# A two-layer hybrid trunk on one core: when modulation, weight splitting and the last output jobs stand in a planned order

## The chip, the cores and the metric

One core of a Trainium2 chip runs one program that holds the whole trunk. The metric is device time in microseconds (us). Engines are named as in the profile: PE is TensorE's matmul side and PEld its weight loads, DVE is VectorE, ACT ScalarE, POOL GpSimd, SP SyncE, whose queue issues nearly every DMA.

## What is computed

2048 rows of width 1024 pass two layers (batch 1). Each layer normalises and modulates its input, projects it, runs two mixers, projects the concatenated result back, normalises that and adds it through a gate:

```python
c_act = jax.nn.silu(c)
for i in range(2):
    shift, scale, gate = split(c_act @ ada_w[i] + ada_b[i], 3)
    h = rms_norm(x, norm_pre[i]) * (1 + scale) + shift
    if i == 0: y = concat([rwkv7_mix(...), short_conv_mix(...)]) @ ev_w_out
    else:      y = concat([conformer_conv_mix(...), mamba2_ssd_mix(...)]) @ od_w_out
    x = x + gate * rms_norm(y, norm_post[i])
```

`rwkv7_mix` is a recurrence over positions (computed in chunks of 64), `conformer_conv_mix` a causal convolution of 31 taps with a layer norm behind it, `mamba2_ssd_mix` a chunked scan. All is float32. A matmul of full accuracy is made of three fast ones: both operands are split into a high part and a rest, and high x high, high x rest and rest x high are added up.

## The kernel before

**Tiling.** The rows are cut into four blocks of 512. Layer 0 has 33 projection jobs for each block and layer 1 has 25; each layer also has 32 output jobs, for an output projection of 16 row tiles by 2 column halves. A job is one PSUM tile `pp` of 128x512 and 24 matmuls (3 products x 8 slices of the inner dimension; the dt job has 16). PE works through a written list of jobs; every other piece of work (evacuations, the recurrences, transposes, norms, loads) is spread between the matmuls.

**The planner.** A single-threaded Python planner emits the instructions in program order. All side work sits in generators in eight queues (`bg`, `quick`, `ev`, `aux`, `post`, `tail`, `urgent`, `slow`); `tick` gives each one step every 2 matmuls in layer 0 and every 4 in layer 1. `later(n, f)` puts a store off by n ticks. In layer 0 (`gated`) a `Clock` models when each engine would be done: `now` is the matmuls' time, `chain` the end of the latest chain, and every DMA issue adds 3.5 us to `chain`; the next matmul starts at the later of the two. A queue's step is held while the engines' modelled lag behind `now` is above a bound (`LAG`, 2 to 3 us; `SLOWV`, 8 us, for the slow queue).

**The work that the change touches.** `modulation` loads a 128x1024 tile of `ada_w` (tile `h`), multiplies it with silu(c) and sums it on DVE into one column of `mod`, followed by one or two 128x1 operations. The first 16 tiles are done in `first_block`; the other 32 (8 for layer 0's gate, 24 for layer 1) are in the slow queue. `gate_row` turns the gate's column into the row tile `gp` that output jobs multiply with. `presplit` reads layer 1's input weights and both layers' output weights, splits them (ACT casts, POOL subtracts) and stores both parts in DRAM (`wo`, `w1`, `wdt`), from where later jobs load them ready. `w_out` loads 16 parts of output weights of one column half into one of two big `act` tiles, as 8 DMAs of 512 KB. `out_jobs` evacuates output jobs: the first half of a row tile is kept in DRAM (`od`), the second fetches it and the row tile `x`, norms, adds and stores. `hblock` norms and transposes the next block's input. `conf_out` ends the conformer branch of a block: four transposes of the convolved channels (`co`) with statistics, four transposes back (`xn`), and per channel group a scaled copy `cs`, a tanh `pr`, two products on DVE, a cast `yh`, and the store of both parts to DRAM as `y`, from which the output jobs of that block load their operand `w`. In the last block the order ends with output jobs of tiles 8 to 11, then of tiles 12 to 15, which need that block's own `y`.

**What sets the order.** The order of jobs is written out by hand in `tile_trunk` (`put` places a list behind the n-th projection job of a block); where a side step lands between them follows from the queues, the clock, and waits for a tile to come free (`take`, which makes the planner wait until `free`; tiles taken from a pool without it make the issuing engine wait on the chip).

Of the kernel before, what the change touches and what calls it, by code (L numbers as in the profile page):

```python
# [9 lines left out]
F32 = mybir.dt.float32  # L10
# [8 lines left out]
P = 128  # L19
D = 1024  # L20
KT = D // P
HALF = 1024
BL = 512
# [125 lines left out]
class Trunk:  # L149
# [83 lines left out]
    def take(self, name, shape, bufs=1, busy=None, dtype=F32):  # L233

        ring = self.rings.setdefault((id(self.t) if name != "tr" else 0, name), [])
        while len(ring) >= bufs and id(ring[-bufs]) in self.inuse:
            yield busy
        t = self.tr.tile(shape, F32, name=name) if name == "tr" else self.t.tile(shape, dtype, name=name, bufs=bufs)
# [27 lines left out]
    def setup(self):  # L266
# [46 lines left out]
        self.kept, self.parted = set(), set()  # L313
# [27 lines left out]
    def gate_row(self, l):  # L341
# [7 lines left out]
        for hb in range(2):  # L349
            ps = yield from self.take("tr", [P, BL], 2)  # L350
# [83 lines left out]
    def run_jobs(self, order, feed):  # L434

        more = lambda n: any(not callable(o) and o[2] == order[n][2] for o in order[n + 1:])
        for n, o in enumerate(order):
# [16 lines left out]
            feed.fetch()  # L454
            if job.mm:
# [210 lines left out]
    def out_jobs(self, l, ts, dh, key):  # L666

        def evac(t, ps):
# [4 lines left out]
            else:  # L673
                x = self.x_rows(l, t, self.xp.tile([P, D], F32, name="x"))
# [35 lines left out]
            def store():  # L710
                self.nc.sync.dma_start(out=self.x1[t] if l == 0 else self.out[t * P:(t + 1) * P], in_=x)
                self.x_done[l].add(t)

# [570 lines left out]
    def conf_out(self, b, st):  # L1284
# [24 lines left out]
        for g in range(4):  # L1309
# [4 lines left out]
            w = yield from self.take("cs", [P, BL])  # L1314
# [239 lines left out]
def tile_trunk(ctx, tc, I, out, T):  # L1554
# [3 lines left out]
    with ExitStack() as e:  # L1558
# [6 lines left out]
        k.slow += [k.modulation(0, range(16, 24), 1), k.modulation(1, range(24), 1), k.gate_row(0)]  # L1565
# [16 lines left out]
        split_w = [(I["w_in1"][j], k.w1[j]) for j in range(24)] + [(I["w_in1"][24], k.wdt)]  # L1582
        put(blocks[1], 0, [lambda: k.slow.append(k.presplit(split_wo(0) + split_w + split_wo(1)))])
# [12 lines left out]
        for b, (l, ts) in enumerate([(0, tiles(2)), (0, tiles(3)), (1, tiles(0)), (1, tiles(1))]):  # L1596
            last = b == NB - 1
            load, jobs = zip(*[outs(l, ts if not dh or not last else range(4, 4 * NB), dh) for dh in range(2)])
            for p, o in zip(at, [load[0], *jobs[0], load[1], *jobs[1][:4]]):
                put(blocks[b], p, [o])  # L1600
            if not last:
# [64 lines left out]
```

## Time and profile before

| | |
|---|---|
| median of 3 runs | 2455.23 us (2452.19 to 2456.57) |
| the profiled execution's own time | 2446.16 us |
| its span | 2444.4 us, mean granted clock 0.947 |
| PE busy | 2208.9 us, 90% of the span, 13408 matmuls |
| PEld busy | 1728.7 us, 71% |
| DVE busy | 1753.1 us, 72% |
| ACT busy / POOL busy | 811.4 us, 33% / 593.3 us, 24% |
| first matmul of each block of layer 0 | 25.6, 364.9, 693.7, 1007.1 us |
| first matmul of each block of layer 1 | 1404.7, 1646.1, 1867.2, 2089.5 us |

Read it as an engine that is nearly always busy, PE, with the time between its busy stretches gathered in a few stages; those stages, not the shares over the whole span, decide what a change is worth. "Granted clock" is the share of TensorE's full clock.

### The profile page before, as it was taken

Reading aid. Unit: us, or ns where it says so; the run is one execution under the profiler, and the core shown is the slowest. Engines: PE = TensorE matmul, PEld = TensorE weight load, DVE = VectorE, ACT = ScalarE, POOL = GpSimd, SP = SyncE. Lnnn points to the kernel's source line nnn. Section 1 sums busy time; section 2 is a strip of 40 time slices with the busy share of each in tenths; the row PEclk is TensorE's granted clock in tenths of the full one; section 3 lists DMA queues with packets and bytes.
Section 4 is the critical chain, followed back from the end, with each engine's and each line's share of the span. In section 5 each row is a group of like instructions: output and inputs, shape, how many; then the busy total and the mean of one; then the engine's idle time right before and its main releaser. Section 6 shows DMA issues by size and latency. Waiting matters only on the chain. (4 is left out here: it accounts for less than half of the span.)

```text
span 2444.4 us, 36532 instructions
## 1 busy us (share of the span) xinstructions
PE 2208.9 (90%) x13408; PEld 1728.7 (71%) x13408; DVE 1753.1 (72%) x3340; ACT 811.4 (33%) x1731; POOL 593.3 (24%) x792
## 2 busy tenths in 40 slices
PE   6688889898988989989999979999999999999957
PEld 4566667676766767667777667877778787878836
DVE  6797897867857778565377443689589859967961
ACT  4334223433233322221222432353443525252221
POOL 2544535335253140221042310210020012002021
PEclk9788989999898999999999989999999999999978
DMA  8675676776776544544788678867877786787756
GB/s 302 223 254 179 216 260 226 234 251 226 248 237 215 199 122 159 190 129 139 254 292 268 235 266 296 301 226 254 293 252 248 243 298 207 267 275 276 244 178 232
DMA packets 232390, 575.18 MB, mean 235 GB/s; under 512 B 20498, under 2 KB 70418, under 8 KB 232212
## 3 DMA queue, kind: packets, MB, share of 16 engines
q1 hardware_dynamic: 232068, 572.59, 69.2%
q8 instruction: 106, 1.74, 0.3%
q14 instruction: 72, 0.59, 0.1%
q10 hardware_dynamic: 144, 0.26, 0.0%
HBM read 436.91 MB, written 135.86 MB: 234 GB/s over the span
## 5 line engine op out<-in xcount | busy, mean ns | idle before, releaser
L111 PE MATMUL pp<-act,w 128*128 128x512 f32 x7000 | 1797.8, 408 | 47.0 <-DMA w<-y 22.0
L111 PEld LDWEIGHTS pp<-act,w 128*128 128x128 f32 x7000 | 1312.5, 193 | 343.5 <-DMA w<-y 22.4
L111 DVE SCALAR_TENSOR_TENSOR co<-u,cfw,co 128x512 f32<-128x512 f32 x480 | 345.3, 754 | 6.1 <-ACT co L111 5.8
L111 POOL TENSOR_SCALAR ss<-ss 128x1 f32<-128x1 f32 x80 | 27.0, 338 | 639.5 <-DVE ss L111 463.2
L111 POOL TENSOR_TENSOR x<-x 128x512 fp32r<-128x512 f32 x80 | 109.0, 1376 | 134.8 <-ACT x L111 134.2
L111 POOL TENSOR_SCALAR sp<-S,PL 128x64 f32<-128x64 f32 x128 | 66.2, 531 | 194.1 <-DVE S L111 193.8
L111 DVE TENSOR_TENSOR pr<-X,BK 128x2 f32<-128x2 f32 (+30 forms) x248 | 101.6, 410 | 6.2
L111 ACT ACTIVATE tA<-pp 128x512 f32<-128x512 f32 x64 | 38.1, 596 | 203.4 <-PE pp L111 201.5
L111 POOL TENSOR_TENSOR w<-x,w 128x512 fp32r<-128x512 f32 x57 | 83.6, 1479 | 56.6 <-ACT w L111 56.4
L111 DVE TENSOR_REDUCE X<-pr 128x1 f32<-128x2 f32 (+30 forms) x248 | 86.5, 349 | 6.1
L111 ACT ACTIVATE q<-pp,cp 128x512 f32<-128x512 f32 x65 | 44.7, 688 | 128.6 <-PE pp L111 106.8
L111 DVE TENSOR_TENSOR UV<-ch,scal 64x128 f32<-64x128 f32 x128 | 36.9, 289 | 58.3 <-PE ch L111 56.3
L111 POOL COPY q<-carry 128x1 f32<-128x1 f32 (+1 forms) x84 | 38.6, 460 | 155.0 <-DVE tG L111 65.0
L111 POOL COPY carry<-q 128x1 f32<-128x1 f32 (+1 forms) x84 | 22.3, 265 | 221.8 <-ACT q L111 172.3
L111 POOL TENSOR_TENSOR x<-x,yo 128x512 f32<-128x512 f32 x32 | 48.5, 1516 | 104.0 <-DVE yo L111 91.5
L111 DVE TENSOR_TENSOR ss<-oss 128x1 f32<-128x1 f32 x32 | 6.0, 189 | 92.1 <-ACT tA L111 92.0
L111 ACT CAST x<-x 128x512 fp32r<-128x512 f32 x80 | 46.6, 616 | 72.6 <-DMA w<-w 19.5
L111 DVE SCALAR_TENSOR_TENSOR tG<-pp,derived,q 128x512 f32<-128x512 f32 x65 | 48.4, 744 | 30.9 <-ACT q L111 30.5
L111 DVE TENSOR_TENSOR act<-tr,act 128x256 fp32r<-128x256 f32 (+1 forms) x120 | 51.3, 436 | 24.1 <-ACT act L111 23.4
L111 PE MATMUL tr<-cc,h 128*128 128x128 f32 x224 | 39.6, 293 | 31.8 <-ACT h L111 28.6
L111 DVE STREAM_TRANSPOSE BK<-SC 32x1024 f32<-32x1024 f32 x32 | 63.8, 1993 | 0.5
L111 ACT ACTIVATE yo<-pp 128x512 f32<-128x512 f32 x32 | 19.1, 597 | 127.9 <-PE pp L111 112.6
(273 smaller groups left out, 3164.6 us busy)
## 6 DMA issues: line engine op xcount, KB each, us to landing
w<-w SPq DMA_DIRECT2D x450, 512.0 KB, 4.3
w<-y SPq DMA_DIRECT2D x128, 512.0 KB, 4.4
act<-wo SPq DMA_DIRECT2D x88, 512.0 KB, 6.1
x<-in_w_in_dram SPq DMA_DIRECT2D x58, 512.0 KB, 5.5
w<-x SPq DMA_DIRECT2D x96, 256.0 KB, 3.4
h<-in_ada_w_dram SPq DMA_DIRECT2D x32, 512.0 KB, 4.9
y<-yh SPq DMA_DIRECT2D x64, 256.0 KB, 3.1
wo<-x SPq DMA_DIRECT2D x64, 256.0 KB, 3.5
```

The lines of the kernel that those rows point to most:

```text
L111: return f(*args, **kw)
```

## The change

Seven edits:

1. `take` handles the `x` tiles (2 buffers), which `presplit` and the second halves of output jobs now take and free, so that the planner waits for one.
2. `presplit` puts its four stores off by 8 ticks (`later(STORE, ...)`), and works on one weight tile at a time.
3. `run_jobs` sets the clock's `chain` back to 0 ahead of each job's matmuls, so that the 3.5 us of a weight fetch no longer move the modelled matmuls.
4. The 32 slow modulation tiles and layer 0's `gate_row` start in block 1, behind the first 21 items of `presplit`; the rest of `presplit` follows them. The order of `presplit` is now: layer 0's output weights, dt, input weights 16 to 23, 12 to 15, then 0 to 11, then layer 1's output weights.
5. `gate_row` waits for a PSUM tile in another way (`busy` True).
6. `conf_out`'s tile `cs` has two buffers.
7. In layer 1's last block, four output jobs (tiles 4 to 7, first half) stand inside the block where there were eight; twelve output jobs (tiles 8 to 11 of half 0, 4 to 11 of half 1) stand between its last projection job and the eight of tiles 12 to 15, where there were eight. One load of output weights (`again`) goes.

```diff
     def take(self, name, shape, bufs=1, busy=None, dtype=F32):
-        ring = self.rings.setdefault((id(self.t) if name != "tr" else 0, name), [])
+        ring = self.rings.setdefault((id(self.t) if name not in ("tr", "x") else 0, name), [])
...
     def presplit(self, tiles):
         for src, parts in tiles:
-            lo = self.raw(src)
+            lo = yield from self.take("x", [P, D], 2)
+            self.nc.sync.dma_start(out=lo if len(src.shape) == 2 else lo.rearrange("p (k t) -> p k t", k=src.shape[1]), in_=src)
...
-            hi = self.xp.tile([P, D], F32, name="x")
+            hi = yield from self.take("x", [P, D], 2)
             yield True
-            yield
             for z in range(2):
                 own = slice(z * BL, (z + 1) * BL)
                 self.split(hi[:, own].bitcast(F32R), lo[:, own].bitcast(F32R), lo[:, own])
-                yield
-            for z in range(2):
-                for i, part in enumerate((hi, lo)):
-                    self.nc.sync.dma_start(out=parts[z][:, i], in_=part[:, z * BL:(z + 1) * BL])
-                self.parted.add(id(parts[z]))
+            def store(parts=parts, hi=hi, lo=lo):
+                for z in range(2):
...
+                self.stored += 1
+                self.free(hi)
+                self.free(lo)
+            self.later(STORE, store)
+            self.begun_split += 1
+            yield
+            while self.stored < self.begun_split:
                 yield
@@ run_jobs
             feed.fetch()
+            self.clock.chain = 0.0
             if job.mm:
@@ out_jobs
-                x = self.x_rows(l, t, self.xp.tile([P, D], F32, name="x"))
+                x = self.x_rows(l, t, (yield from self.take("x", [P, D], 2, "blocked")))
@@ conf_out
-            w = yield from self.take("cs", [P, BL])
+            w = yield from self.take("cs", [P, BL], 2)
@@ tile_trunk
-        k.slow += [k.modulation(0, range(16, 24), 1), k.modulation(1, range(24), 1), k.gate_row(0)]
...
-        put(blocks[1], 0, [lambda: k.slow.append(k.presplit(split_wo(0) + split_w + split_wo(1)))])
+        put(blocks[1], 0, [lambda: k.slow.extend(
+            [k.presplit(split_wo(0) + split_w[:13]), k.modulation(0, range(16, 24), 1), k.modulation(1, range(24), 1), k.gate_row(0), k.presplit(split_w[13:] + split_wo(1))])])
...
-        again, first = outs(1, range(8, 4 * NB), 0)
-        blocks[-1] += [again, *jobs[1][4:8], *first[:4]] + [j for two in zip(jobs[1][8:], first[4:]) for j in two]
+        load, jobs = zip(*[outs(1, range(4, 4 * NB), dh) for dh in range(2)])
+        for p, o in zip((1, 5, 10, 15, 18), [load[0], *jobs[0][:4]]):
+            put(blocks[-1], p, [o])
+        blocks[-1] += [load[1], *jobs[0][4:8], *jobs[1][:8]] + [j for two in zip(jobs[0][8:], jobs[1][8:]) for j in two]
```

**DVE, block 0, the chain ahead of its first recurrence step.** `h,mod_107<-h,gp` is one modulation tile, `tG`, `tA` and `wal` belong to the recurrence's preparation. Before:

```order
L111 SCALAR_TENSOR_TENSOR h,mod_107<-h,gp 128x1024
L111 SCALAR_TENSOR_TENSOR tG<-yp,derived,q 128x512
L111 TENSOR_TENSOR mod_107<-mod_107,cp 128x1
L111 TENSOR_TENSOR gs_109<-mod_107,cp 128x1
L111 SCALAR_TENSOR_TENSOR h,mod_107<-h,gp 128x1024
L111 TENSOR_TENSOR mod_107<-mod_107,cp 128x1
L111 TENSOR_TENSOR gs_109<-mod_107,cp 128x1
L111 SCALAR_TENSOR_TENSOR h,mod_107<-h,gp 128x1024
L111 TENSOR_TENSOR wal_865<-w2a_832,wh_863 64x128
```

Of the change, the same place:

```order
L111 SCALAR_TENSOR_TENSOR tD<-tG,cp,tD 128x512
L111 TENSOR_SCALAR scal<-kss 64x2 x4
L111 SCALAR_TENSOR_TENSOR tG<-yp,derived,q 128x512
L111 TENSOR_TENSOR wal_852<-w2a_845,wh_850 64x128
L111 TENSOR_TENSOR wal_852<-w2a_845,ah_851 64x128
L111 TENSOR_SCALAR tA<-tA 128x512
L111 SCALAR_TENSOR_TENSOR tA<-reset,tA 128x512
```

The modulation tiles between `tG` and `wal` are gone. Before, 31 of the 32 stand in block 0 and one at the start of block 1; now 8 stand in block 1 and 24 in block 2. With them `gate_row(0)` moves from the first jobs of block 1 to the end of block 2. Elsewhere in layer 0 few instructions change their places on DVE and ACT; the splits of layer 1's output weights now end ahead of the last layer 0 job instead of among layer 1's first jobs, and 56 small matmuls of layer 0's recurrence and its transposes stand behind the last layer 0 job instead of 16.

**PE, the end of the last block.** `co` and `xn` are `conf_out`'s transposes, `act_61` and `act_62` the two operand tiles of output weights and of the block. Before, from the last of the eight jobs that stood ahead of tiles 12 to 15:

```order
L111 MATMUL pp<-act_62,w 128x512 x18
L111 MATMUL tr<-cc,co 128x128 x2
L111 MATMUL pp<-act_62,w 128x512 x12
L111 MATMUL tr<-cc,co 128x128 x4
L111 MATMUL pp<-act_62,w 128x512 x10
L111 MATMUL tr<-cc,co 128x128 x4
L111 MATMUL tr<-cc,xn 128x128 x16
L111 MATMUL pp<-act_61,w 128x512 x24
```

Of the change:

```order
L111 MATMUL tr<-cc,co 128x128 x4
L111 MATMUL pp<-act_62,w 128x512 x20
L111 MATMUL tr<-cc,xn 128x128 x4
L111 MATMUL pp<-act_62,w 128x512 x12
L111 MATMUL tr<-cc,xn 128x128 x4
L111 MATMUL pp<-act_62,w 128x512 x12
L111 MATMUL tr<-cc,xn 128x128 x4
L111 MATMUL pp<-act_62,w 128x512 x24
L111 MATMUL tr<-cc,xn 128x128 x4
L111 MATMUL pp<-act_62,w 128x512 x44
L111 MATMUL pp<-act_61,w 128x512 x24
```

The four groups of `xn` transposes stood in one bunch with no output job between them or behind them; now 112 matmuls of output jobs stand between the last `co` and the first job (`act_61`, the last row) that needs the block's own `y`.

**ACT, the same place.** `cs`, `pr` and `yh` are the three ACT operations per channel group, `tA,oss` an output job's second half. Before:

```order
L111 ACTIVATE tA,oss<-pp 128x512 x4
L111 ACTIVATE cs<-tr,cp 128x512
L111 ACTIVATE pr<-tr,derived 128x512
L111 CAST yh<-cs 128x512
L111 ACTIVATE cs<-tr,cp 128x512
L111 ACTIVATE pr<-tr,derived 128x512
L111 CAST yh<-cs 128x512
```

Of the change:

```order
L111 ACTIVATE tA,oss<-pp 128x512 x4
L111 ACTIVATE cs<-tr,cp 128x512
L111 ACTIVATE pr<-tr,derived 128x512
L111 ACTIVATE cs<-tr,cp 128x512
L111 CAST yh<-cs 128x512
L111 ACTIVATE pr<-tr,derived 128x512
L111 ACTIVATE tA,oss<-pp 128x512
L111 CAST yh<-cs 128x512
L111 ACTIVATE tA,oss<-pp 128x512 x2
```

The second `cs` now stands ahead of the first `yh`, and evacuations of output jobs stand between the groups.

## Rows read from the trace of the kernel before

**Rows 1.** The page's 40 slices of the span: busy tenths and granted clock.

```profile
PE   6688889898988989989999979999999999999957
DVE  6797897867857778565377443689589859967961
PEclk9788989999898999999999989999999999999978
```

**Rows 2.** Windows by stage: us; busy of PE, PEld, DVE, ACT, POOL; clock; DMA.

```profile
46.00:145.00 99.00, 74.34 (x343) 57.57 (x341) 76.69 (x137) 33.63 (x65) 41.01 (x45) 0.76 0.70 254
145.00:198.00 53.00, 44.98 (x240) 36.97 (x241) 48.60 (x102) 18.95 (x35) 22.79 (x23) 0.89 0.72 257
198.00:307.00 109.00, 98.79 (x809) 72.96 (x808) 91.33 (x191) 45.20 (x92) 56.42 (x68) 0.94 0.57 191
307.00:365.00 58.00, 46.86 (x262) 37.29 (x261) 56.81 (x122) 13.02 (x25) 18.46 (x17) 0.87 0.76 266
365.00:694.00 329.00, 303.03 (x2403) 226.83 (x2401) 245.69 (x499) 105.57 (x195) 130.04 (x166) 0.94 0.72 238
694.00:1007.00 313.00, 287.56 (x2128) 217.06 (x2126) 225.17 (x462) 88.61 (x164) 87.90 (x130) 0.93 0.55 179
1007.00:1405.00 398.00, 378.20 (x2685) 288.98 (x2680) 245.88 (x508) 109.44 (x212) 95.14 (x153) 0.97 0.65 219
1405.00:1490.00 85.00, 68.44 (x275) 53.85 (x275) 35.23 (x64) 30.48 (x73) 13.64 (x10) 0.86 0.78 269
...
2341.00:2390.00 49.00, 11.89 (x52) 8.28 (x51) 21.53 (x37) 9.63 (x16) 8.74 (x15) 0.63 0.45 146
2390.00:2436.00 46.00, 45.93 (x192) 37.54 (x192) 6.88 (x12) 7.16 (x18) 6.09 (x9) 0.95 0.73 262
```

**Rows 3.** DVE groups by shape, 95 to 385 us: count | busy us, mean ns.

```profile
L111 DVE SCALAR_TENSOR_TENSOR h<-h,gp 128x1024 f32<-128x1024 f32 x31 | 43.0, 1388 | 7.0 <-DMA h<-in_ada_w_dram 7.0
L111 DVE TENSOR_TENSOR mod<-mod,cp 128x1 f32<-128x1 f32 x31 | 12.8, 414 | 0.1
L111 DVE TENSOR_TENSOR gs<-mod,cp 128x1 f32<-128x1 f32 x15 | 4.5, 300 | 0.1
L111 DVE SCALAR_TENSOR_TENSOR gs<-mod,cp 128x1 f32<-128x1 f32 x8 | 3.0, 378 | 0.0
```

**Rows 4.** Tiles h and mod, 90 to 390 us: ns min/median/max, first and last start.

```profile
L111 DVE SCALAR_TENSOR_TENSOR h<-h,gp x31: 1161/1216/2335, 94.5 to 378.8; 128x1024 f32<-128x1024 f32 x31
L111 DVE TENSOR_TENSOR mod<-mod,cp x31: 105/152/1247, 96.4 to 380.8; 128x1 f32<-128x1 f32 x31
```

**Rows 5.** POOL groups by shape, 95 to 385 us, the largest.

```profile
L111 POOL TENSOR_TENSOR w<-x,w 128x512 fp32r<-128x512 f32 x50 | 74.0, 1492 | 52.5 <-ACT w L111 52.4
```

**Rows 6.** PE's waits, 25 to 365 us, the largest: us in total, times, longest.

```profile
PE tr L111 <- DVE tE L111: 18.7, 2, 10.7
```

**Rows 7.** PE's waits, 365 to 1405 us, first and last of the eleven over 1.5 us.

```profile
PE tr L111 <- DVE yy L111: 16.0, 4, 6.3
...
PE tr L111 <- DVE kss L111: 1.6, 1, 1.6
```

**Rows 8.** PE's waits, 1405 to 1490 us.

```profile
PE tr L111 <- DMA x<-in_w_out_dram: 6.9, 1, 6.9
PE pp L111 <- DMA w<-w: 4.5, 2, 3.0
```

**Rows 9.** Tile S, 1300 to 1405 us: 16 of its DVE updates, two a step.

```profile
L111 DVE SCALAR_TENSOR_TENSOR S<-ch,PL,sp x16: 273/276/285, 1339.7 to 1373.1; 128x64 f32<-128x64 f32 x16
```

**Rows 10.** ACT's timeline, 2356 to 2384 us: start, us, operation, idle before.

```profile
2358.03 0.78 ACT L111 ACTIVATE cs<-tr,cp 128x512 f32<-128x512 f32 x1 [6.07 <-PE tr L111]
...
2365.47 0.78 ACT L111 ACTIVATE cs<-tr,cp 128x512 f32<-128x512 f32 x1 [3.90 <-DMA y<-cs]
...
2372.35 0.78 ACT L111 ACTIVATE cs<-tr,cp 128x512 f32<-128x512 f32 x1 [3.33 <-DMA y<-cs]
...
2379.28 0.78 ACT L111 ACTIVATE cs<-tr,cp 128x512 f32<-128x512 f32 x1 [3.34 <-DMA y<-cs]
```

**Rows 11.** PE's timeline, 2340 to 2391 us: the last row.

```profile
2390.07 1.22 PE L111 MATMUL pp<-act,w 128*128 128x512 f32 x2 [21.98 <-DMA w<-y]
```

**Rows 12.** DVE's timeline, 2300 to 2346 us: the convolution's taps.

```profile
2305.42 24.97 DVE L111 SCALAR_TENSOR_TENSOR co<-u,cfw,co 128x512 f32<-128x512 f32 x37
...
2343.47 0.74 DVE L111 SCALAR_TENSOR_TENSOR co<-u,cfw,co 128x512 f32<-128x512 f32 x1
```

More of the change, by code (lines that the diff above doesn't have):

```diff
@@ L233, in take @@
     def take(self, name, shape, bufs=1, busy=None, dtype=F32):
-        ring = self.rings.setdefault((id(self.t) if name != "tr" else 0, name), [])
+        ring = self.rings.setdefault((id(self.t) if name not in ("tr", "x") else 0, name), [])
         while len(ring) >= bufs and id(ring[-bufs]) in self.inuse:
             yield busy
-        t = self.tr.tile(shape, F32, name=name) if name == "tr" else self.t.tile(shape, dtype, name=name, bufs=bufs)
+        t = {"tr": self.tr, "x": self.xp}[name].tile(shape, F32, name=name) if name in ("tr", "x") else self.t.tile(shape, dtype, name=name, bufs=bufs)
         ring.append(t)
@@ L349, in gate_row @@
         for hb in range(2):
-            ps = yield from self.take("tr", [P, BL], 2)
+            ps = yield from self.take("tr", [P, BL], 2, True)
             for q in range(4):
@@ L410, in presplit @@
                 self.split(hi[:, own].bitcast(F32R), lo[:, own].bitcast(F32R), lo[:, own])
-                yield
-            for z in range(2):
-                for i, part in enumerate((hi, lo)):
-                    self.nc.sync.dma_start(out=parts[z][:, i], in_=part[:, z * BL:(z + 1) * BL])
-                self.parted.add(id(parts[z]))
+            def store(parts=parts, hi=hi, lo=lo):
+                for z in range(2):
+                    for i, part in enumerate((hi, lo)):
+                        self.nc.sync.dma_start(out=parts[z][:, i], in_=part[:, z * BL:(z + 1) * BL])
+                    self.parted.add(id(parts[z]))
+                self.stored += 1
+                self.free(hi)
+                self.free(lo)
+            self.later(STORE, store)
+            self.begun_split += 1
+            yield
+            while self.stored < self.begun_split:
                 yield
@@ L712, in store @@
                 self.x_done[l].add(t)
+                self.free(x)
             self.later(STORE, store)
@@ L1595, in tile_trunk @@
         at = 1, 3, 5, 7, 9, 9, 12, 13, 15, 16
[L1596 to L1599, printed above, removed]
+        for b, (l, ts) in enumerate([(0, tiles(2)), (0, tiles(3)), (1, tiles(0))]):
+            load, jobs = zip(*[outs(l, ts, dh) for dh in range(2)])
+            for p, o in zip(at, [load[0], *jobs[0], load[1], *jobs[1]]):
                 put(blocks[b], p, [o])
-            if not last:
-                put(blocks[b], at[-1], ahead(1, b + 1, 2))
+            put(blocks[b], at[-1], ahead(1, b + 1, 2))
             if b == 1:
                 put(blocks[1], 23, [lambda: k.slow.append(k.gate_row(1))])
-        again, first = outs(1, range(8, 4 * NB), 0)
-        blocks[-1] += [again, *jobs[1][4:8], *first[:4]] + [j for two in zip(jobs[1][8:], first[4:]) for j in two]
+        load, jobs = zip(*[outs(1, range(4, 4 * NB), dh) for dh in range(2)])
+        for p, o in zip((1, 5, 10, 15, 18), [load[0], *jobs[0][:4]]):
+            put(blocks[-1], p, [o])
+        blocks[-1] += [load[1], *jobs[0][4:8], *jobs[1][:8]] + [j for two in zip(jobs[0][8:], jobs[1][8:]) for j in two]
         order1 = sum(blocks, [])
```

4 lines of the change are left out of this document (2 added, 2 removed).

## The prediction

> **What bounds the kernel now.** I read the page's slices first: PE is at 8 or 9 tenths almost everywhere, except in the first four slices and in the last two [rows 1]. So PE bounds the kernel, and time can be won only where PE is idle or runs at its low clock. Then I cut the span into stages [rows 2] and compared, for each, its length with PE's busy time multiplied by the granted clock, which is what the same matmuls would take at the full one of the two levels (2.4 GHz).
>
> Block 0, from 46 to 365 us, lasts 319 us. PE is busy for 265.0 us of it, which at full clock would be 74.3 x 0.76 + 45.0 x 0.89 + 98.8 x 0.94 + 46.9 x 0.87 = 230 us. DVE is busy for 273.4 us, 86%: more than PE [rows 2]. Blocks 1 and 2 last 329 and 313 us for 284.8 and 267.4 us at full clock, 1.155 and 1.17 times; there DVE stands idle for 83 and 88 us [rows 2]. Block 3 lasts 1.085 times its full-clock time (398 over 366.9). In blocks 1 to 3 PE waits 67.4 us in the eleven rows over 1.5 us, led by transposes that wait for DVE or ACT [rows 7], and the low clock costs it 303.0 + 287.6 + 378.2 - 919.1 = 50 us more. Layer 1 is at full clock with little idle time, so that nothing is to be had there until the tail: between 2341 and 2390 us PE works 11.9 us at 0.63, so 49 - 7.5 = 41.5 us are lost, 22 of them in one wait for the reload of the block's own `y` [rows 2, 11].
>
> **Block 0 loses 32 modulation tiles.** They cost DVE 43.0 + 12.8 + 4.5 + 3.0 = 63.3 us there and 7 us of waiting for the `ada_w` loads at the head of its queue [rows 3]. Behind them in DVE's order stand the recurrence's preparation and the evacuations, on which PE waits (18.7 us for `tE` alone [rows 6]). If block 0 then ran like blocks 1 and 2, at 1.16 times its full-clock time, it would last 267 us: -52. If DVE's load was not what held it (the start-up chains are), 0. I take **-40**: DVE at 86% is nearer to the first, but in the first 99 us PE's clock is 0.76 and DVE is busy for only 77 us, which speaks for chains that stay.
>
> **The same tiles in blocks 1 and 2.** They add between 51 us (32 x 1.6 us, by the medians of the two main operations, 1.216 and 0.152 us, and as much again for the third) and 65 us (32 x 2.04, by the means) to DVE [rows 3, 4], against its idle 83 and 88 us [rows 2]. Most of it, 24 tiles, lands in block 2, where DVE goes from 225 to some 265 us of about 300. Hidden entirely it costs 0, not at all 65. Block 0 at 86% DVE shows that it is not free, block 1 at 75% runs at 1.155: **+15**. Their 32 loads (512 KB, 16.8 MB) go by SP's queue in blocks where DMA is busy 0.72 and 0.55; the 12.6 MB of block 2 on top of 313 us x 179 GB/s = 56 MB lift 0.55 to 0.67, less than block 1 bears today [rows 2]. They are no term.
>
> Why the mean and the median differ is a place to weigh a rule. The multiplication takes 1.16 to 2.34 us and the 128x1 addition 0.105 to 1.25 us [rows 4], while POOL splits weights beside them for 74 us [rows 5]. The Trainium skill ("SBUF — State Buffer", "Who interferes with whom") says that a DVE instruction with two SBUF inputs and a GpSimd instruction that reads SBUF exclude each other for a whole instruction. By that rule the moved tiles, which stand in one queue with `presplit` and never beside its subtracts, would cost 51 us, and the term would be 15 x 51/65 = 12, the sum 3 us less; the spread of the rows agrees with it, but the jobs' own splits go on beside them, so I keep 15.
>
> **The clock leaves fetches out.** Before, each job's fetch moved the modelled matmuls 3.5 us on, so in layer 0 the planner thought that DVE was less behind than it was and let more steps through; PE then waited for them. Now steps are held to LAG of matmul time. That can give back up to 67 us, the waits of blocks 1 to 3 [rows 7]; or nothing, where these waits are dependences that stand too close whatever the pace (each recurrence step is 4.5 us: 16 updates, two a step, in 33.4 us [rows 9]). Few instructions of layer 0 move on DVE and ACT apart from the modulation, so I take **-20**.
>
> **`presplit`.** Same reads, subtracts and stores; its `x` tile no longer makes SP's queue wait with its stores at the head. It ends ahead of layer 1. In the first 85 us of layer 1, PE's idle 16.6 us hold a wait of 6.9 us that is named by an output-weight load and 3.0 us for a weight fetch [rows 2, 8]: **-10** (0 if these only change their names). Against that, 40 more small matmuls of layer 0's recurrence stand behind its last job: two steps at 4.5 us and as long again for its output: **+13** (0 if layer 1's first jobs cover them, 20 if a third step waits). Together +3.
>
> **The tail.** `cs` waits in each of its three later rounds for the DMA store of the round before, 3.90, 3.33 and 3.34 us [rows 10]: with a second buffer these **10.6 us** go. And four output jobs leave the block for the place behind it: 4 x 5.75 = 23 us (192 matmuls in 46 us are eight jobs [rows 2]). The convolution's taps (0.675 us each, 37 in 24.97 us [rows 12]) run on DVE behind the last projections, so they end **23 us** earlier against PE's end, and twelve jobs cover what eight did. Less: second halves of four tiles now come behind the last projection instead of ahead, each two DVE products and an addition, at about 0.7 us by a tap of the same shape [rows 12]: some +9 on DVE in the convolution's time, of which I count a third, **+3**. -10.6 - 23 + 3 = **-31** of the 41.5 lost. Ends: -15 (only the second buffer and some cover), -41.5 and 2 more of the low clock at 0.95 behind it [rows 2]. The load of output weights that goes (8 x 512 KB) is hidden on SP: 0.
>
> **Sum.** The profiled execution took 2446.16 us: -40 + 15 - 20 + 3 - 31 = -73 gives 2373.2. The median of the runs is 9.1 us above that execution, and a forecast is for a median: 2382. `take` for `x` in output jobs and `gate_row`'s busy wait have no term: PE waits for neither tile in layer 1 in the windows above.
>
> **The rivals.**
> - *The waits of blocks 1 to 3 go nearly whole* (-67 in place of -20): 2382 - 47 = 2335. For it speaks that their releasers are DVE and ACT [rows 7], which a slower pace relieves; against it that the dependences stay. Chance 0.12.
> - *Block 2 becomes bound by DVE*, and the moved tiles cost all 65 us: 2382 + 50 = 2432. For it speaks block 0, with DVE at 86%; against it that DVE would have 265 of 300 us, with less bunched work. 0.15.
> - *The tail's gain goes to another wait*: the layer norm's chain (PE, DVE, POOL, PE, ACT, DVE, ACT, DMA, DMA) now shares ACT and DVE with twelve evacuations, and each group takes as long as a round took (7.1 us [rows 10]). 2382 + 31 = 2413. 0.10.
> - *The change doesn't do what it says*: with the honest clock the planner holds the recurrence back further, its rest stands uncovered at the layer change, and the -20 is not won but the drain costs 13 more: 2382 + 20 + 13 = 2415. 0.06.
> - *Slower*: block 0 was held by its start-up chains, its DVE time was free (0 in place of -40), and the 65 us cost in full in blocks 1 and 2, where PE is 0.92 busy and everything lies close: 2382 + 40 + 50 = 2472 and up to 2492 without the -20. It decides where the price in blocks 1 and 2 exceeds the gain in block 0 by more than the 48 us that the tail, the clock and the layer change give. 0.06.
> - Something between the second rival and the last, within 0.2% of before (2450 to 2460, about what a measurement of this kernel can tell from no change): 0.03.
>
> That leaves **0.48** for the forecast (its own range 2355 to 2405). The range reaches from the first rival's 2335 to a little over the second: **2332 to 2438**. Outside lie half of the first rival, the last two and a part of the second, under 2 in 10. Faster 0.91, same 0.03, slower 0.06.
>
> **What would show it.** Right: no `h<-h,gp` tiles in block 0 and its 319 us near 280; the same tiles, with a mean nearer to 1.2 than to 1.4 us, between 500 and 950 us; DVE in block 2 over 260 us busy and PE waits there not above those of before; the last wait for `w<-y` under 5 us; ACT's `cs` rows without a wait for `y<-cs`. Wrong: block 0 still over 310 us (then the chains held it); blocks 1 and 2 together over 690 (then DVE binds them); more than 15 us of PE idle time ahead of the last eight jobs.

## The result and the profile after

The changed kernel takes 2376.97 us (median of 4 runs, 2371.24 to 2379.3) against 2454.56 us: 0.9681 of the time, 95% interval 0.9661 to 0.970. The forecast was 2382 with a range from 2332 to 2438. The sum held to 5 us, but not its terms: one was several times too large, one left out half of what it stands for, and they made up for each other. That is luck, and the rest of this document is about it.

Where the time went is read first from the blocks. This table gives, for each kernel that ran, the time from the first matmul of a block's first job to that of the next block's, in us of its profiled execution; the last column runs to the last matmul. "Layer 0" is the sum of its four blocks.

| kernel | block 0 | 1 | 2 | 3 | layer 0 | layer 1: 0 | 1 | 2 | 3 and tail |
|---|---|---|---|---|---|---|---|---|---|
| before | 339.3 | 328.8 | 313.4 | 397.6 | 1379.1 | 241.4 | 221.2 | 222.2 | 346.6 |
| changed | 319.4 | 297.0 | 327.2 | 395.5 | 1339.1 | 232.5 | 220.5 | 224.4 | 323.8 |
| e1_clock_alone | 324.6 | 341.1 | 282.8 | 474.2 | 1422.7 | 223.9 | 220.6 | 223.8 | 348.6 |
| e2_mod_block1 | 332.1 | 320.8 | 317.7 | 486.3 | 1456.9 | 224.2 | 221.7 | 224.8 | 347.5 |
| e3_tail_alone | 340.7 | 328.7 | 313.3 | 397.4 | 1380.1 | 237.8 | 221.3 | 223.0 | 322.7 |
| e4_split_alone | 341.1 | 325.3 | 316.1 | 399.4 | 1381.9 | 225.0 | 222.3 | 225.0 | 348.4 |
| e5_clock_and_need | 326.8 | 334.4 | 297.6 | 396.7 | 1355.5 | 279.0 | 222.1 | 224.2 | 346.9 |
| e6_mod_in_block0 | 325.5 | 331.6 | 307.3 | 388.5 | 1352.9 | 233.4 | 220.1 | 225.2 | 329.6 |
| e7_no_clock | 332.6 | 311.6 | 333.3 | 400.7 | 1378.2 | 223.7 | 221.8 | 227.5 | 323.8 |
| e8_one_cs | 323.2 | 295.6 | 329.6 | 394.6 | 1343.0 | 232.7 | 220.9 | 224.6 | 344.9 |
| e9_cs3 | 317.4 | 299.6 | 326.9 | 392.6 | 1336.5 | 234.1 | 221.0 | 222.6 | 317.6 |
| e10_cs3_store3 | 317.5 | 296.7 | 331.4 | 394.5 | 1340.1 | 232.6 | 223.2 | 223.9 | 316.7 |
| e11_cs3_late_clock | 324.3 | 296.1 | 336.6 | 413.5 | 1370.5 | 224.4 | 220.8 | 223.5 | 320.9 |
| e12_mod_twice | 328.7 | 297.5 | 341.6 | 388.8 | 1356.6 | 234.8 | 222.9 | 223.7 | 323.2 |

By this table the change is worth 40 us in layer 0, 9 in the first block of layer 1 and 23 in the last block and the tail, 70 in all with the two blocks between. The medians differ by 78: the kernel before was profiled in an execution 8.4 us below its median, the changed one within 1 us of its own. Other rows stand up to 9 us off as well (e6 and e11 9 above their medians, e8 6 above, e3 and e9 6 below), so small differences between rows are weighed by the runs too. The page's slices of the changed kernel answer to [rows 1]:

```profile
PE   6798899899998998999999979999999999999977
DVE  6596787787977889586468453699589848987961
PEclk9799999999999999999999999999999999999998
```

The clock's dips in the first eight slices are gone but one, and the last two hold 7 and 7 where there were 5 and 7. The windows by stage, cut at the changed kernel's own blocks (columns as in [rows 2]):

```profile
46.00:145.00 99.00, 82.08 (x374) 64.98 (x373) 67.74 (x139) 42.54 (x85) 40.02 (x52) 0.83 0.60 223
145.00:345.00 200.00, 179.00 (x1272) 138.31 (x1271) 159.82 (x300) 70.44 (x135) 90.04 (x104) 0.93 0.57 199
345.00:642.00 297.00, 280.91 (x2064) 209.80 (x2063) 236.37 (x493) 99.36 (x184) 109.39 (x149) 0.97 0.73 243
642.00:969.00 327.00, 303.67 (x2266) 228.42 (x2266) 265.58 (x559) 98.35 (x182) 117.14 (x146) 0.93 0.75 249
969.00:1364.50 395.50, 382.19 (x2807) 291.18 (x2807) 243.74 (x502) 104.91 (x202) 91.42 (x156) 0.98 0.66 221
...
2232.00:2319.30 87.30, 70.09 (x322) 56.87 (x321) 64.90 (x104) 19.01 (x41) 20.44 (x32) 0.93 0.89 310
2319.30:2365.80 46.50, 46.44 (x192) 37.86 (x192) 6.89 (x12) 7.18 (x19) 6.51 (x10) 0.94 0.85 295
```

In block 0 (first two rows) DVE is busy for 227.6 us, 46 less than before, and the block is only 20 us shorter: DVE's load went, but PE's idle time fell only from 54 to 38 us. In block 2 DVE has the 265 us that were forecast. The moved tiles themselves, tile h (min/median/max, first and last start; answers to [rows 4]), and DVE's group (count | busy us, mean ns; answers to [rows 3]):

```profile
L111 DVE SCALAR_TENSOR_TENSOR h<-h,gp x32: 1204/1214/2308, 495.2 to 919.5; 128x1024 f32<-128x1024 f32 x32
```

```profile
L111 DVE SCALAR_TENSOR_TENSOR h<-h,gp 128x1024 f32<-128x1024 f32 x32 | 40.5, 1268 | 0.4 <-DMA h<-in_ada_w_dram 0.3
```

The mean fell from 1388 to 1268 ns, and the wait for the loads from 7 us to 0.4. PE's waits from 345 to 1364 us (answers to [rows 7]; first three of eleven over 1.5 us):

```profile
PE tr L111 <- ACT BKT L111: 8.4, 2, 5.7
PE tr L111 <- DVE act L111: 7.2, 3, 5.8
PE tr L111 <- DVE bv L111: 6.3, 3, 4.7
```

The eleven sum to 48.1 us where there were 67.4, 19 less (and 64.9, in fifteen rows, in the changed kernel without the clock's reset, e7 below), and what the low clock costs in the three blocks falls from 50 to 280.9 x 0.03 + 303.7 x 0.07 + 382.2 x 0.02 = 37 us.

The tail, in ACT's timeline from 2278 to 2322 us (start, us, operation, idle before; answers to [rows 10]):

```profile
2283.31 0.78 ACT L111 ACTIVATE cs<-tr,cp 128x512 f32<-128x512 f32 x1 [2.63 <-PE tr L111]
...
2286.51 0.78 ACT L111 ACTIVATE cs<-tr,cp 128x512 f32<-128x512 f32 x1 [1.75 <-PE tr L111]
...
2294.38 0.60 ACT L111 ACTIVATE tA<-pp 128x512 f32<-128x512 f32 x1 [2.98 <-PE pp L111]
...
2300.32 0.60 ACT L111 ACTIVATE tA<-pp 128x512 f32<-128x512 f32 x1 [5.25 <-PE pp L111]
...
2300.91 0.77 ACT L111 ACTIVATE cs<-tr,cp 128x512 f32<-128x512 f32 x1
...
2302.23 0.78 ACT L111 ACTIVATE cs<-tr,cp 128x512 f32<-128x512 f32 x1
```

No copy waits for a store any more. But the third stands in ACT's order behind two evacuations (`tA`) that wait for PE's output jobs, and starts at 2300.91 although its transposes were issued at 2289.10 and took 0.6 us. PE's timeline shows that, and what it costs (answers to [rows 11]):

```profile
2289.10 0.60 PE L111 MATMUL tr<-cc,xn 128*128 128x128 f32 x4
...
2295.04 0.60 PE L111 MATMUL tr<-cc,xn 128*128 128x128 f32 x4
...
2319.31 10.86 PE L111 MATMUL pp<-act,w 128*128 128x512 f32 x35 [13.65 <-DMA w<-y]
```

The wait for the reload of `y` is 13.6 us where it was 22.0, and PE is idle for 17.2 us of the last 87 before the final eight jobs. Before, PE also waited 7.0 us for ACT's `pr` and 5.8 for DVE's `xn` ahead of the transposes; of these 1.8 us are left. The three waits together make 19 of the tail's 23 us.

### The profile page after: what moved, and what is told of

The parts are those of the page before. It is cut to its first block, busy times and chain, and to the rows that moved or that the text cites. A ratio compares the mean times of both kernels' runs of the same rounds, so it can differ in the third digit from the quotient of the medians.

```text
span 2374.4 us, 36508 instructions
## 1 busy us (share of the span) xinstructions
PE 2200.2 (93%) x13408; PEld 1725.4 (73%) x13408; DVE 1738.1 (73%) x3340; ACT 812.7 (34%) x1731; POOL 577.7 (24%) x792
## 5 line engine op out<-in xcount | busy, mean ns | idle before, releaser
L111 PE MATMUL pp<-act,w 128*128 128x512 f32 x7000 | 1779.0, 405 | 29.9 <-DMA w<-y 13.6
L111 POOL TENSOR_TENSOR x<-x 128x512 fp32r<-128x512 f32 x80 | 114.3, 1446 | 162.2 <-ACT x L111 144.2
L111 DVE TENSOR_TENSOR pr<-X,BK 128x2 f32<-128x2 f32 (+30 forms) x248 | 107.5, 433 | 6.3
L111 POOL TENSOR_SCALAR sp<-S,PL 128x64 f32<-128x64 f32 x128 | 74.6, 596 | 130.8 <-DVE S L111 129.8
L111 POOL TENSOR_TENSOR w<-x,w 128x512 fp32r<-128x512 f32 x57 | 78.8, 1389 | 75.2 <-ACT w L111 69.6
L111 ACT CAST act<-tr 128x256 fp32r<-128x256 f32 (+1 forms) x120 | 45.6, 392 | 41.9 <-DVE tr L111 40.3
L111 PE MATMUL tr<-AR,BK 64*128 64x128 f32 x512 | 52.1, 301 | 7.9 <-DVE SC L111 3.4
L111 ACT CAST w<-x 128x512 fp32r<-128x512 f32 (+1 forms) x61 | 36.9, 623 | 65.7 <-PE pp L111 44.3
L111 POOL TENSOR_SCALAR bmv<-bmv 128x1 f32<-128x1 f32 x16 | 5.3, 330 | 220.1 <-DVE bmv L111 216.2
```

What stands on the lines that cost most here:

```text
L111: return f(*args, **kw)
```

## The experiments

**One edit at a time, on the kernel before.** The first four runs ask which edit carries which of the table's gains.

e1: the clock alone.

```diff
             feed.fetch()
+            self.clock.chain = 0.0
```

> The kernel before with edit 3 alone (the clock leaves fetches out). My theory: the steps of layer 0 are held to true matmul time, PE's waits for DVE and ACT in blocks 1 to 3 shrink, so 10 to 30 us faster (2425 to 2445), with blocks 1 to 3 together under 1030 us (1040 before) and block 0 within 5 us of 339. Rival (the clock does nothing of use; block 1 became 32 us shorter only because modulation, the gate row and the splits moved): within 5 us of before. Second rival (the order is held back too far): layer 0 longer by 10 us or more.

Measured: 2476.03 us against 2456.13, ratio 1.0093 (1.0075 to 1.011): slower. My theory is out and so is the first rival. The second rival, that work is held back too far, fits: layer 0 is 44 us longer. But it is not spread over the layer. Blocks 0 and 2 are 15 and 31 us shorter, block 1 12 longer, and block 3 77 longer. Nearly all of that lies at its last job, which lasts 88.4 us to the first matmul of layer 1 (13.0 before). The window there:

```profile
1362.00:1450.00 88.00, 17.10 (x159) 12.31 (x158) 20.44 (x52) 23.92 (x50) 27.20 (x28) 0.58 0.70 241
```

No engine is busy for even a third of it. The next job, dt, needs `wdt`. Tile wdt of this kernel (one store: ns min/median/max, first and last start):

```profile
L111 SPq DMA_DIRECT2D wdt<-w x1: 327/327/327, 1439.3 to 1439.3; - x1
```

and of the kernel before:

```profile
L111 SPq DMA_DIRECT2D wdt<-w x1: 319/319/319, 1292.7 to 1292.7; - x1
```

`presplit` does dt's tile behind 32 others. Before, its store had a margin of some 110 us ahead of layer 1; in e1 the splits aren't done when layer 0 is, and the planner steps through the rest of them with PE idle.

What holds the splits is to be read from SP's queue. They share the two buffers of tile `x` with the row tiles that second halves of output jobs fetch, and a split needs both. The kernel before (SP's timeline from 800 to 830 and from 1236 to 1262 us; `w<-x` is a store of a split, `x<-in_x_dram` the fetch of a row tile, `x<-x` its store when the job is done):

```profile
818.17 0.45 SPq L111 DMA_DIRECT2D w<-x  x1
821.82 0.33 SPq L111 DMA_DIRECT2D x<-in_x_dram  x1
...
1246.42 0.32 SPq L111 DMA_DIRECT2D x<-x  x1
...
1250.09 2.23 SPq L111 DMA_DIRECT2D w<-x  x3
```

Between 818 and 1250 us no split is stored: one row tile, fetched some 420 us ahead of its use, stops them, with 120 of their 161 stores done. In e1 the first row tile comes at 702.8 us (first start of 16; tile x):

```profile
L111 SPq DMA_DIRECT2D x<-in_x_dram x16: 332/378/1003, 702.8 to 1804.4; - x16
```

Its store goes out at 1217.2 us, and the splits stand still from 702.0 to 1223.0 us with 84 stores done. Up to there they are hardly slower than before (the 84th store came at 682 us). So what the reset changed for them is that fewer were written ahead of the first row tile; that held steps in the slow queue are the reason follows from the planner's rules and was not tested apart.

e2: modulation out of block 0 alone, in its plainest form.

```diff
-        k.slow += [k.modulation(0, range(16, 24), 1), k.modulation(1, range(24), 1), k.gate_row(0)]
...
-        put(blocks[1], 0, [lambda: k.slow.append(k.presplit(split_wo(0) + split_w + split_wo(1)))])
+        put(blocks[1], 0, [lambda: k.slow.extend([k.modulation(0, range(16, 24), 1), k.modulation(1, range(24), 1), k.gate_row(0), k.presplit(split_wo(0) + split_w + split_wo(1))])])
```

> The kernel before with the modulation move alone, in its simplest form: the 32 tiles and the gate row come at the start of block 1, ahead of the splits, all else as before. My theory (DVE's load in block 0 costs about a third of its 63 us there): block 0 about 20 us shorter (319), and block 1, which now takes all 32 tiles, 15 to 30 us longer; in all within 10 us of before. Rival (block 0 is held by start-up chains, and its 20 us come from the clock or the splits): block 0 within 5 us of 339, the whole 15 to 50 us slower.

Measured: 2511.1 us, 1.0248 (1.0224 to 1.0273): slower by 61 us, more than the rival's 50 and for another reason. Block 0 gains 7 us, not 20. But the edit does only in part what it was meant to. Tile h:

```profile
L111 DVE SCALAR_TENSOR_TENSOR h<-h,gp x32: 1182/1218/2206, 234.3 to 629.6; 128x1024 f32<-128x1024 f32 x32
```

Ten of the 32 tiles start ahead of block 1's first matmul (357.5 us), although the planner writes them behind block 0's last job: an engine's order on the chip isn't in all places the order of writing, and why is not shown here. Block 1, which takes in the other 22, doesn't get longer (320.8 against 328.8). The loss is again the layer change: the last job of layer 0 lasts 90.7 us, with `wdt` stored at 1473.5 us. The splits stand behind the modulation in the slow queue; on the chip their first store is earlier than before (343.3 against 379.1 us), but only 84 of 161 are done when the first row tile is fetched (746.4 us), and the next comes at 1244.2 us.

e3: the tail alone (edits 6 and 7; the diff is theirs).

> The kernel before with edits 6 and 7 alone (second cs buffer, last block's order). My theory: the tail is a stage of its own, so 20 to 26 us faster, as block 4 of layer 1 and what follows went from 346.5 to 323.8 us with all edits; layer 0 as before within 3 us. Rival (part of the tail's gain needs the x tiles taken by the planner or the changed layer 0): 10 us or less.

Measured: 2426.76 us, 0.9894 (0.9873 to 0.9915), 26 us by the ratio; the last block and the tail fall from 346.6 to 322.7 us, layer 0 stands within 1 us. A stage of its own, as expected.

e4: edits 1, 2 and 5 alone (`take` for the x tiles, the stores put off, the gate row's wait).

> The kernel before with edits 1, 2 and 5 alone (x tiles taken and freed, the stores of presplit put off, the gate row's wait). My theory: these only take waits out of SP's queue and end the splits a little ahead of layer 1, so 0 to 10 us faster, of it most in the first block of layer 1 (241.4 us before, 232.5 with all edits). Rival (they carry block 1's 32 us): 20 us or more faster, block 1 under 310 us. Second rival (one tile at a time is too slow, and the output weights come late for the jobs that need them): slower by 5 us or more.

Measured: 2437.07 us, 0.9935 (0.9915 to 0.9954): 16 us by the ratio, more than I gave them. Layer 0 is unchanged (1381.9 against 1379.1), so the rival that they carry block 1's gain falls; the whole of it is the first block of layer 1, 241.4 to 225.0. The splits' last store, in tile wo of this kernel (first and last start):

```profile
L111 SPq DMA_DIRECT2D wo<-x x64: 319/320/949, 380.9 to 946.0; - x64
```

It stands at 946 us; in the kernel before the same row ends at 1471.5 us, inside layer 1. So these edits bring the splits' end half a millisecond ahead. The first row tile of an output job is fetched behind it:

```profile
L111 SPq DMA_DIRECT2D x<-in_x_dram x16: 332/360/493, 950.4 to 1765.9; - x16
```

and no two stores of the splits are more than 32 us apart, where there was a halt of 432 us. Of the three edits, the first bears on that, since the planner now waits for an `x` tile on behalf of both users; the three were not run apart.

The ratios of e1 to e4 add up to +0.93% + 2.48% - 1.06% - 0.65% = +1.7%; together the edits give -3.2%. The four are not quite the change's parts, as e2 leaves out the order of need, but e5 (below) finds that order worth little without the quicker splits: the change is not a sum of its parts.

e5: does the order of need alone rescue the clock?

```diff
+            self.clock.chain = 0.0
...
-        split_w = [(I["w_in1"][j], k.w1[j]) for j in range(24)] + [(I["w_in1"][24], k.wdt)]
+        split_w = [(I["w_in1"][24], k.wdt)] + [(I["w_in1"][j], k.w1[j]) for j in (*range(16, 24), *range(12, 16), *range(12))]
```

> The kernel before with edit 3 (the clock) and of edit 4 only the order of need in presplit (dt's tile first of the input weights, then 16 to 23, 12 to 15, 0 to 11); modulation stays in block 0. The clock alone lost some 75 us at the layer change, where layer 1's first job, dt, stood still until its weights were stored at 1439 us (1293 us before). My theory: held steps make the slow queue late, only the dt tile at its end counts, and with it early the rest of the clock's gain appears: 2476 - 75 = about 2400, 2390 to 2415, with the last output job ahead of layer 1 under 20 us. Rival (all the splits are late, and the stall only moves on to the jobs of layer 1 that need the later tiles): over 2430.

Measured: 2464.08 us, 1.003 (1.0015 to 1.0046). The stall at the last job is gone (14.5 us), block 3 is back at 396.7, but the first block of layer 1 takes 279.0 us: the splits run until 1579.3 us, and from 1400 to 1640 us PE is busy for 198 of 240 us. My theory missed by 64 us and the rival was right: all the splits are late, not only dt's, and the stall only moves on. The halt is there as well: 85 of 161 stores are done by 898 us, the first row tile is fetched at 899 us, and the next store comes at 1229 us. The order of need without the quicker splits is worth 12 us of the 75 by the medians, 15 by the ratios.

**One edit taken back, in the changed kernel.**

e6: modulation and the gate row in block 0 again.

```diff
+        k.slow += [k.modulation(0, range(16, 24), 1), k.modulation(1, range(24), 1), k.gate_row(0)]
...
-            [k.presplit(split_wo(0) + split_w[:13]), k.modulation(0, range(16, 24), 1), k.modulation(1, range(24), 1), k.gate_row(0), k.presplit(split_w[13:] + split_wo(1))])])
+            [k.presplit(split_wo(0) + split_w + split_wo(1))])])
```

> The changed kernel with the 32 modulation tiles and the gate row at the start again (in block 0), all else as changed. The prediction's step (-40 in block 0, +15 in blocks 1 and 2): about 2402. Revised theory after the first runs (block 0 gives only 7 us for the tiles, its other 13 come from the clock; blocks 0 to 2 together took 948.5 us with the clock alone and 943.6 us with everything): 2375 to 2387. Rival (the move is what keeps the splits from piling up): slower by over 25.

Measured: 2387.64 us, 0.9732 (0.9707 to 0.9757). The move is worth some 11 us: the prediction's 25 is out, the revised theory's upper end was missed by 0.6 us. With the honest clock the tiles don't even fit into block 0: 23 of the 32 start there, the last at 411.4 us, and the gate row behind it; block 1 is 34.6 us longer than in the changed kernel, and blocks 2 and 3 give 27 of that back.

e7: no reset of the clock.

```diff
             feed.fetch()
-            self.clock.chain = 0.0
```

> The changed kernel without edit 3 (a fetch moves the modelled matmuls again). The prediction's step (-20): 2397. Revised theory (the clock gave block 0 its 15 us and blocks 1 and 2 some 20 us, once nothing waits at the layer change): 2405 to 2420, block 0 over 330 us. Rival (the clock gives nothing beside the other edits): within 5 us of 2377.

Measured: 2407.51 us, 0.9799 (0.9775 to 0.9822): the clock is worth 30 us, as revised and more than the prediction's 20. By the table it gives 39 us in layer 0 (1378.2 to 1339.1) and takes 9 at the layer change (223.7 to 232.5).

e8: one `cs` buffer.

```diff
-            w = yield from self.take("cs", [P, BL], 2)
+            w = yield from self.take("cs", [P, BL])
```

> The changed kernel with one cs buffer. The prediction's step (10.6 us for three rounds): about 2388, the wait for the reload of y 10 us longer than 13.6. Rival (with twelve jobs behind the block the rounds have cover, and the buffer matters little): within 3 us of 2377. Second rival: the planner's own wait puts each copy behind further output jobs, and the wait grows by over 15 us.

Measured: 2395.63 us, 0.9739 (0.9712 to 0.9767), 19 us by the medians. PE's wait for the reload:

```profile
PE pp L111 <- DMA w<-y: 27.8, 1, 27.8
```

14 us longer, in between the theory's 10 and the second rival's 15; by the ratios the run is 14 us slower. ACT's later three copies (its timeline from 2295 to 2350 us) show both reasons:

```profile
2312.71 0.77 ACT L111 ACTIVATE cs<-tr,cp 128x512 f32<-128x512 f32 x1
...
2325.82 0.78 ACT L111 ACTIVATE cs<-tr,cp 128x512 f32<-128x512 f32 x1 [6.91 <-DMA y<-cs]
...
2334.92 0.78 ACT L111 ACTIVATE cs<-tr,cp 128x512 f32<-128x512 f32 x1 [4.13 <-DMA y<-cs]
```

The third and the fourth wait for a store again, 11 us together, as the prediction has it. The second stands behind three output jobs' evacuations and starts 14 us after its transposes (2298.18 us): that is the planner's wait. With two buffers it was the third copy that stood so.

**A third buffer, a shorter delay, a later clock, more DVE work.** The last four runs test what is left.

e9: `take("cs", [P, BL], 3)`.

> The changed kernel with three cs buffers. One buffer less cost 19 us, so the planner's wait for a free copy is what sets the tail. Theory (the third copy no longer waits, and the fourth still stands behind the same three evacuations in ACT's order, since its buffer is the first one's): 0 to 4 us faster, the wait for the reload of y from 13.6 to 9 to 13 us. Rival (every buffer gives as much as the second): 10 us or more faster, 2367 or less.

Measured: 2372.94 us, 0.966 (0.9634 to 0.9685). 4 us by the medians, at the end of the forecast; its interval overlaps the changed kernel's. The wait shows the effect itself, and is a little shorter than was forecast:

```profile
PE pp L111 <- DMA w<-y: 8.4, 1, 8.4
```

The third copy now starts at 2287.46 us, right behind its transposes, and the fourth, at 2298.63 us, behind two evacuations: the copy beyond the buffers is the late one each time.

e10: as e9, and in `y_store`:

```diff
-        self.later(STORE, store)
+        self.later(STORE if l == 0 else 3, store)
```

> As e9, and layer 1's y stores put off by 3 ticks instead of 8. Theory (in the tail the two last stores stand behind two other transfers in SP's queue and 5 ticks of 4 matmuls, 5 us, too late): the wait for the reload of y falls by another 4 to 8 us, 2362 to 2372 in all. Rival (with a shorter delay SP's queue waits with a store at its head for the cast or the subtraction, and holds back the weight fetches of layer 1's other blocks): no faster than e9, blocks 1 to 3 of layer 1 longer by 2 us or more each.

Measured: 2369.29 us, 0.9635 (0.961 to 0.9661). The wait is 7.9 us, hardly less than e9's, so that the shorter delay gives next to nothing: the expected 4 to 8 us didn't come. Blocks 1 and 2 of layer 1 are 2.2 and 1.3 us longer and the last no longer, which is within the blocks' scatter, so the rival isn't shown either. It is still the lowest median of all that ran, not to be told from e9's; its interval touches the changed kernel's at 0.9661, with the third buffer as the part that a wait shows.

e11: the reset only up to layer 0's last 58 entries.

```diff
-            self.clock.chain = 0.0
+            if n < len(order) - 58:
+                self.clock.chain = 0.0
```

> As e9, with the clock's reset only up to the last 58 entries of layer 0's list, its last block, where fetches move the clock again as before. Without the reset anywhere the first block of layer 1 took 223.7 us instead of 232.5, and block 3 some 5 us more. Theory (the 9 us at the layer change are the price of holding recurrence steps back in the last block): layer 1's first block at 224 to 227 us, block 3 within 6 us of 395, in all 2 to 6 us faster than e9. Rival (the steps held back come from blocks before, and pile up in block 3 itself): block 3 over 403 us, no gain.

Measured: 2386.56 us, 0.9718 (0.9689 to 0.9748), 14 us slower than e9. Half of the theory holds: layer 1's first block is at 224.4 us again. But block 3 takes 413.5 us and block 2 336.6 (the 58 entries reach back over its last six jobs, and most of its loss is in the last two of them), and the rival is right in its numbers: block 3 alone pays twice what the next stage gets. The 9 us at the layer change are the price of a better block 3.

e12: the product of a modulation tile done twice.

```diff
             self.mod_tile(l, j, r)
+            self.nc.vector.scalar_tensor_tensor(out=r, in0=r, scalar=0.5, in1=self.cact, op0=ALU.mult, op1=ALU.mult, accum_out=self.mod[n][:, c:c + 1])
             yield
```

> The changed kernel with the 128x1024 product of 31 of the 32 slow modulation tiles done a second time on DVE, the second result unused: 31 x 1.35 us = 42 us more of DVE's work in blocks 1 and 2 (the planner counts it as work). The prediction's step (23% of the tiles' time shows): +8 to +12 us, 2385 to 2390. Rival (blocks 1 and 2 are bound by DVE): +30 us or more. Second rival (hidden): within 3 us of 2377.

The second sum goes into the next tile's column, which that tile overwrites. Measured: 2395.24 us, 0.9744 (0.9717 to 0.9772), 18 us by the medians and 4 to 27 by the ends of the intervals. Tile h:

```profile
L111 DVE SCALAR_TENSOR_TENSOR h<-h,gp x63: 1189/1216/2302, 504.3 to 945.8; 128x1024 f32<-128x1024 f32 x63
```

In the profile, blocks 1 to 3 take 1027.9 us against 1019.7, so 8 of the added work's 38.5 us (the group's busy time is 79.0 us, 40.5 in the changed kernel) show in the blocks that the work stands in; 9 more are in block 0, whose program is the same as the changed kernel's (below). Whether a fifth or nearly a half of such work shows is open; that all of it does, is not: the rival of 30 us or more is out, and, just, the one of 3.

## Why the prediction was right, and where it wasn't

**The signs.** Most of those that were to show it right came: the tiles stand between 495 and 920 us with a mean of 1.27 us, DVE is busy for 265.6 us in block 2 with PE idle for 23 us there (25 before), and no `cs` copy waits for a store. Two did not: from 46 us on block 0 lasts 299 us, not near 280, and the last wait for `w<-y` is 13.6 us, not under 5. One sign of being wrong is there: PE is idle for 17.2 us ahead of the last eight jobs, over the 15 that were named.

**What bounds the kernel: right.** PE does, with time to be won in layer 0 and the tail; nothing moved in blocks 1 and 2 of layer 1.

**Block 0, -40 for 32 tiles: wrong, the mechanism and the size.** The same block was run with both edits on and off, in several kernels each (two profiles at least):

| block 0, us | old clock | clock reset |
|---|---|---|
| tiles written in block 0 (30 of 32 start there, 23 with the reset) | 339.3, 340.7, 341.1 | 324.6, 326.8, 325.5 |
| tiles moved out (none starts there, ten in the 332.1 of e2) | 332.1, 332.6 | 319.4, 323.2, 317.4, 317.5, 324.3, 328.7 |

The tiles are worth 8 us with the old clock and 4 with the new one, on the means, and the 4 are hardly more than the scatter of the last cell; the clock is worth 15 us with the tiles there, where it also puts seven of them out of the block, and 11 without. Even the 8 are a fifth of the 40. The step that failed was to read DVE at 86% busy as the bound, against the clause in the prediction itself that the start-up chains hold the block: DVE lost 46 us of work there and PE got 20 back, most of them from the pace at which steps are let through. The lower end of the price, 0, was nearer than the end that I leaned to.

**The moved tiles in blocks 1 and 2, +15: right in kind, too large.** e12 shows such work hidden for the greater part, and without the clock blocks 1 to 3 together are 6 us longer than before (e7, 1045.6 against 1039.8). (The 51 us of the working, by the medians, add up to 49: 1.52 us a tile.) That e6 is 11 us slower than the changed kernel says that the whole move is worth -11, where the prediction had -40 + 15 = -25. Without the clock it is worth nothing: e7's layer 0 takes 1378.2 us against 1379.1 before, and e2's without its stall, as far as the stall can be taken off, 1456.9 - 77.7 = 1379.2.

The exclusion of DVE and GpSimd that the Trainium skill states ("SBUF — State Buffer", "Who interferes with whom") would have had the moved tiles shed their long cases. The mean fell from 1388 to 1268 ns, 4 us over 32 tiles, of the right sign. By the two traces, eight of the 32 tiles took over 1.3 us before and three do now, up to 2308 ns. Each of the eleven has a `TENSOR_TENSOR` of POOL beside it, which for the three is no split but a product of the recurrence's preparation (tile `BK`), and no tile without POOL beside it took over 1.23 us. But several with POOL at work beside them took 1.2 us as well, and no run here separates the port from anything else that could stretch an instruction.

**The clock, -20: right in its mechanism, mis-sized because a place was left out.** PE's waits in blocks 1 to 3 fell by 19 us, as said. But the same pace works in block 0, which the prediction didn't count, and over layer 0 the term is -39: 13 in block 0 and 26 in blocks 1 to 3 (e7). And the rival that spoke against it, that the planner holds work back until it stands uncovered, was true as well, in two places: 9 us at the layer change in the changed kernel, and 75 us when nothing else is changed (e1), where the held work is the splits. I had priced that at 13, for the recurrence.

**`presplit`, 3 for both sides: mis-sized.** Edits 1, 2 and 5 give 16 us (e4), not 10, and the steps behind layer 0 cost 9, not 13: -7 by these runs, and -9 in the table, where +3 was said. What no term said is that these edits carry the clock: e5, with the clock and the order of need but the old splits, loses 38 us in that block. The prediction gave `take` for `x` no term because PE waits for neither tile in layer 1. The one that waited was `presplit`, in layer 0: one output job's row tile held a buffer for some 420 us and stopped the splits from 818 to 1250 us, with no line of its own among PE's waits.

**The tail, -31: right in its mechanism, 23 measured.** One of its parts was taken for another: a `cs` buffer is worth 14 to 19 us (e8), not 10.6, since the planner's `take` puts a copy behind output jobs' evacuations in ACT's order, where it waits for PE. The new order, on the other hand, gives little by itself: with one buffer the last block and the tail take 344.9 us (in a profile 6 us above that kernel's median), 346.6 before, where 20 us were forecast for the twelve jobs' cover. The cover pays only when the copies come early enough to use it; the second buffer without the new order was not run. Of the 13.6 us that remain, 5 are the third copy's (e9); the rest was not traced to its end. The row with `y<-cs` as the releaser showed the wait on the chip, but not where the planner would place the instruction next.

**The sum.** Layer 0: forecast -40 + 15 - 20 = -45, measured -40. The first block of layer 1: +3 and -9. The tail: -31 and -23. In layer 0 about 34 us too much for the tiles in block 0 were covered by some 10 too much for their price in blocks 1 and 2 and 19 too little for the clock. Nor are the terms independent: all but the clock gives layer 0 1 us (e7), all but the move 26 (e6), both 40. So the sum's 5 us say nothing for its terms. What stays open: 6 us of e6's profile lie in the tail (329.6 against 323.8 us), whose jobs are the same; by the runs at hand that is scatter between profiles.

## What to carry to other kernels

In a program whose side work is placed by a modelled clock, an error in the model is not one term but a pace: setting it right gains wherever PE waited, and delays whatever was being let through early. Before such a fix, look for the latest thing that each stage hands to the next (here one 512 KB weight tile with 110 us to spare) and bring it forward first; alone, the fix cost 20 us, and with quicker splits it gave 30. Look also at pools that two kinds of work share: a tile that one of them takes long before it needs it stops the other, and the wait shows in no line of the busiest engine's waits, only as a gap between the other's stores. And an engine's busy share in a stage that begins with dependent steps is no price for work taken off it: vary it with the pace fixed and see.

## What the runs showed that was not expected

Block 0 of the changed kernel, e8 to e12 is the same program up to its last job, and it took 317.4 to 328.7 us in six profiles, while the blocks of layer 1 with equal work agree within some 5 us. In the four of them whose layer 0 is the same throughout (the changed kernel, e8, e9, e10), blocks 1 to 3 agree within 5 us too, and all of layer 0 within 7. So a difference of under 10 us in a block of layer 0 is not read from one profile, and the two-by-two table above rests on its means.
